# Low parts of sixteen weight tiles by a negated copy and an adding DMA, in a hybrid decoder block on one core

## The chip, the cores and the metric

One core of a Trainium2 chip runs the whole kernel in one launch. The metric is the device time in microseconds (us), the median of several executions. A profiled execution gives the trace; its times count from the start of its span.

The engines by the names used here: TensorE (PE) multiplies, and loads its weights beside that (PEld); VectorE (DVE), ScalarE (ACT) and GpSimd (POOL) work element by element; SyncE (SP) issues most transfers. POOL and ACT issue transfers too, each on a queue of its own.

## The reference, cut to what matters

```python
u = rmsnorm(h, g_mix); z = u @ w_in
...
y_a = o @ w_o_nsa                                # o: attention output
y_b = c @ w_conv_out + b_conv_out                # c: convolution branch
h = h + (ga * y_a + gb * y_b) @ w_out
v = rmsnorm(h, g_ffn) @ w_up
v = causal_dwconv(v, ffn_conv_w, ffn_conv_b)
v_gate, v_val = jnp.split(v, 2, axis=-1)
h = h + (jax.nn.gelu(v_gate) * v_val) @ w_down
gate = jax.nn.sigmoid(rmsnorm(h, g_ple) @ w_ple_gate)
h = h + gate * (p @ w_ple)
return rmsnorm(h, g_final)
```

One sequence of 1024 rows, model width 1024, FFN width 2816, p of width 256, all in float32.

## The kernel before, in words

**Products in two parts.** A float32 product is made of fast products of rounded operands. Each operand is split into a high part, its value rounded to the format that PE takes (`F32R`), and a low part, the value minus the high part. Three matmuls follow for each step: high by high, high by low, low by high (`mm3`, and written out with `mm`, line 169). The low part of a weight is so needed by one matmul in three.

**Weights.** A queue of weight tiles is fixed in advance by `add_w`, in the order of their use: 32 tiles of w_in (z), w_conv_out (co), w_o (o, four tiles), p and w_ple (p and pl), and the 22 chunks of the gate half of w_up (up). The tiles here are 128x1024, 512 KB. `w_fetch` (lines 86 to 93) keeps up to two fetches ahead on SP's queue, into a pool `wp` with two buffers for raw tiles (tag "wr"): a third tile can be fetched only when the first has been read. `w_split` (lines 95 to 108) takes a raw tile and makes the parts: one copy on ACT into the high part (line 102), which rounds, and two subtractions of 512 columns, raw minus high, into the low part (lines 103 to 105). These run on `lo_eng[0]`, VectorE at the start and from the end of the attention on, GpSimd during attention. Names in the rows: wr is a raw tile, wh a high part, wl a low part; the high and low parts of most weights have two buffers each (tags "wh" and "wl").

**Stages around the change.** After the attention come y_b and y_a (w_o, eight column chunks in four tiles). Then the product with w_out, in the seven products of a Strassen-like scheme (`o_steps`), with three of the four pieces of p @ w_ple (`pw_steps`, lines 970 to 989) woven between; a piece stores its result with a transfer issued by POOL (pw_d, line 987). `norm_a` makes the sums of squares and scaled rows of the next norm (lines 182 to 187, f in the rows) and stores h (h_d) by POOL; `norm_b` and `norm_c` transpose them on PE (line 198) and split the sums that the seven FFN products need (T and S in the rows, lines 1178 and 1179, 1195 to 1207). Then the FFN up product, chunk after chunk: `gen` makes the operands, `prod` multiplies. The chunks up 0 to up 3 start early, between the norms, with the fourth piece of p @ w_ple after the first of them (`EARLY`, `NE`); from chunk 4 on there is a regular loop. The x rows that `o_steps` loads are f<-in_x_dram; x in the names of PE's rows is an operand of the w_out product.

**What sets the order.** The program is written as calls woven by hand (`weave`), and a scheduler with a timeline of its own then orders the instructions of every engine (`schedule_with_timeline_sim`). Each engine runs its list in order and waits where an operand or a buffer isn't ready.

Of the kernel before, what the change touches and what calls it, by code (L numbers as in the profile page):

```python
# [11 lines left out]
AF = mybir.ActivationFunctionType  # L12
ALU = mybir.AluOpType
# [21 lines left out]
def tile_hybrid_block(ctx: ExitStack, tc: tile.TileContext, a: dict, out: bass.AP):  # L35
    nc = tc.nc
# [9 lines left out]
    def nm(s):  # L46
        cnt[0] += 1
        return f"{s}{cnt[0]}"
# [37 lines left out]
    lo_eng = [nc.vector]  # L86

    def w_fetch():
        while order and len(raws) < AHEAD:
            key, src, n, pl, th, tl = order.pop(0)  # L90
            raw = wp.tile([128, n], F32, tag="wr", name=nm("wr"))
            nc.sync.dma_start(raw if len(src.shape) == 2 else raw.rearrange("p (c n) -> p c n", c=src.shape[1]), src)
            raws.append((key, raw, n, pl, th, tl))

    def w_split():

        w_fetch()
        if raws and raws[0][3] in pools:
            key, raw, n, pl, th, tl = raws.pop(0)
            hi = pools[pl].tile([128, n], F32R, tag=th, name=nm("wh"))  # L100
            lo = pools[pl].tile([128, n], F32R, tag=tl, name=nm("wl"))
            nc.scalar.activation(hi, raw, AF.Copy)  # L102
            for c0 in range(0, n, 512):
                cs = slice(c0, min(c0 + 512, n))
                lo_eng[0].tensor_tensor(lo[:, cs], raw[:, cs], hi[:, cs], op=ALU.subtract)  # L105
            raw_of[key] = raw
            made.append((key, (hi, lo)))

    def w_get(key):
        while not made:  # L110
            assert order or raws, key
            w_split()
        k, w = made.pop(0)
        assert k == key, (k, key)
        return w
# [24 lines left out]
    EARLY, NE = (3,), 4  # L140
# [135 lines left out]
    def zsteps(z, w, th, nk=8, src=None, split=1):  # L276

        wh, wl = w
        srcs = src or u

        def step(k):
            sl = slice(128 * k, 128 * k + 128)
            movs = []
            for h in th:
                hi, lo = srcs[h][k // 2]
                movs.append((hi[:, k % 2], lo[:, k % 2]))
            mm3([z[h] for h in th], wh[:, sl], wl[:, sl], movs, k == 0, k == nk - 1)
            if k == split:
                w_split()

        return [(lambda k=k: step(k)) for k in range(nk)]
# [254 lines left out]
    for j, nk in enumerate((3, 3, 2)):  # L546
        hi, lo = w_get(("v", j))
# [6 lines left out]
    def v_tile(i):  # L554
        zv = tt_()
        th, t0 = divmod(i, 4)
        for k in range(8):
            uh, ul = u[th][k // 2]
            uh = uh[:, k % 2, 128 * t0:128 * t0 + 128]
            ul = ul[:, k % 2, 128 * t0:128 * t0 + 128]  # L560
            mm(zv[:, 0:280], uh, wv[k][0], k == 0, False)
            mm(zv[:, 0:280], uh, wv[k][1], False, False)
            mm(zv[:, 0:280], ul, wv[k][0], False, k == 7)
        if i == 2:
            w_split()
        for g in range(2):
            vsrc = zv[:, 0:256].rearrange("p (b g d) -> p b g d", b=2, g=2)[:, :, g]
            vd = V[g][i // 4][:, i % 4]
            nc.scalar.activation(vd[:, :, 0:64], vsrc, AF.Copy)
            nc.vector.tensor_sub(vd[:, :, 64:128], vsrc, vd[:, :, 0:64])  # L570
        nc.scalar.activation(gts[:, i], zv[:, 256:280], AF.Tanh, scale=0.5)
# [1120 lines left out]
```

## Time and profile before

| | |
|---|---|
| Median of 3 runs | 1578.37 us (1578.05 to 1578.44) |
| Profiled execution | 1580.51 us |
| Its span | 1578.8 us |
| Mean granted clock of PE | 0.997 |
| DVE, ACT, POOL busy | 77%, 49%, 23% of the span |

The profiled execution stands 2.1 us above the median. The span leaves out 1.7 us at its ends. A busy time adds up the stretches in which an engine worked; an instruction's own time can overlap that of the next on the same engine (a 128x512 matmul takes 0.39 us and the next starts 0.23 us after it). A granted clock of 1.00 is the full 2.4 GHz.

### The profile page before, as it was taken

How to read it: one execution, taken by the hardware profiler on the slowest of the kernel's cores; microseconds unless marked ns; L12 is line 12 of the kernel's file. 1: busy time of each engine (PE TensorE's matmuls, PEld its weight loads, DVE VectorE, ACT ScalarE, POOL GpSimd, SP SyncE). 2: the span in 40 equal slices, each digit the busy share in tenths (PEclk: the TensorE clock that was granted, in tenths of full speed). 3: DMA queues.
4: the chain of work that ended last, by engine and by line, in shares of the span. 5: the costliest groups of instructions: out<-in, count | busy, mean ns of one | idle time of the engine just before them, and what ended most of it. 6: DMA issues, size and time to landing. Idle time of an engine off the chain costs nothing. (4 is left out here: it accounts for less than half of the span.)

```text
span 1578.8 us, 22128 instructions
## 1 busy us (share of the span) xinstructions
PE 1543.1 (98%) x7746; PEld 1305.6 (83%) x7746; DVE 1216.5 (77%) x2342; ACT 780.8 (49%) x1472; POOL 358.0 (23%) x402
## 2 busy tenths in 40 slices
PE   9999999999999999999998999999999989999998
PEld 7888889888988898887876888888888867888886
DVE  4999788577764887779779898898879768778554
ACT  5113324467755776614556454454554456554332
POOL 2000004566663576500120111211111100000000
PEclk9999999999999999999999999999999999999999
DMA  4123233211123431465143232232322499454321
GB/s 165 63 97 124 71 122 142 74 54 55 41 95 122 159 134 68 145 229 187 61 179 134 87 114 87 102 125 81 120 107 87 149 328 311 163 175 133 105 76 54
DMA packets 76048, 194.40 MB, mean 123 GB/s; under 512 B 8481, under 2 KB 8865, under 8 KB 75937
## 3 DMA queue, kind: packets, MB, share of 16 engines
q1 hardware_dynamic: 57184, 146.58, 26.5%
q10 hardware_dynamic: 14400, 31.20, 5.3%
q0 software_dynamic: 4352, 15.21, 2.6%
q8 instruction: 61, 1.00, 0.2%
q14 instruction: 51, 0.41, 0.1%
HBM read 140.26 MB, written 52.69 MB: 122 GB/s over the span
## 5 line engine op out<-in xcount | busy, mean ns | idle before, releaser
L169 PE MATMUL t<-T,S 128*128 128x512 f32 x1320 | 310.4, 390 | 2.2 <-DVE T L1179 1.3
L169 PEld LDWEIGHTS t<-T,S 128*128 128x128 f32 x1320 | 247.5, 188 | 55.4 <-DVE T L1179 2.2
L169 PE MATMUL t<-u,wh 128*128 128x512 f32 x1024 | 288.7, 392 | 0.4 <-DVE u L274 0.3
L169 PEld LDWEIGHTS t<-u,wh 128*128 128x128 f32 x1024 | 189.1, 188 | 36.9 <-DVE ms L252 0.6
L169 PE MATMUL t<-wh,a 128*128 128x512 f32 x616 | 191.8, 392 | 4.2 <-ACT wh L1453 4.2
L169 PE MATMUL t<-u,wl 128*128 128x512 f32 x512 | 167.0, 392 | 0.0
L102 ACT ACTIVATE wh<-wr 128x1024 fp32r<-128x1024 f32 (+1 forms) x72 | 75.5, 1050 | 172.6 <-PE t L169 111.5
L707 POOL TENSOR_TENSOR S<-S,r 128x512 f32<-128x512 f32 (+1 forms) x152 | 140.6, 951 | 60.6 <-DVE r L727 39.0
L336 DVE SCALAR_TENSOR_TENSOR s<-s,cw,s 128x1019 f32<-128x1019 f32 (+16 forms) x120 | 151.6, 1267 | 2.9
L169 PEld LDWEIGHTS t<-wh,a 128*128 128x128 f32 x616 | 116.0, 189 | 29.6 <-ACT wh L1453 5.7
L1337 POOL TENSOR_TENSOR f<-f,f 128x1024 f32<-128x1024 f32 x21 | 57.2, 2726 | 358.2 <-DVE f L1367 227.9
L169 PE MATMUL t<-wl,a 128*128 128x512 f32 x308 | 120.4, 393 | 2.5 <-DVE wl L1454 2.5
L169 PE MATMUL t<-T,wh 128*128 128x512 f32 x352 | 112.8, 393 | 2.3 <-ACT S L1202 1.8
L166 DVE TENSOR_TENSOR P<-t,P 128x512 fp32r<-128x512 f32 (+1 forms) x168 | 97.2, 593 | 22.9 <-ACT P L165 22.0
L165 ACT ACTIVATE P<-t 128x512 fp32r<-128x512 f32 (+1 forms) x168 | 84.2, 524 | 53.8 <-PE t L763 44.1
L169 PEld LDWEIGHTS t<-u,wl 128*128 128x128 f32 x512 | 95.4, 188 | 18.5
L169 PE MATMUL t<-P,v 128*128 128x256 f32 x528 | 102.9, 296 | 0.5 <-ACT P L165 0.2
L722 ACT ACTIVATE S<-S,ngm 128x640 f32<-128x640 f32 (+7 forms) x128 | 93.1, 732 | 13.7 <-DVE ngm L717 13.5
L1297 ACT ACTIVATE S<-s 128x512 fp32r<-128x512 f32 x88 | 54.3, 627 | 76.0 <-PE t L169 47.9
L105 DVE TENSOR_TENSOR wl<-wr,wh 128x512 fp32r<-128x512 f32 x108 | 70.8, 696 | 25.6 <-ACT wh L102 25.3
L169 PE MATMUL t<-v,v 128*128 128x512 f32 (+1 forms) x408 | 89.6, 378 | 0.0
L1458 ACT ACTIVATE a<-r 128x512 fp32r<-128x512 f32 x77 | 48.5, 631 | 82.0 <-PE t L169 59.6
(257 smaller groups left out, 2986.5 us busy)
## 6 DMA issues: line engine op xcount, KB each, us to landing
r<-a_d SPq DMA_DIRECT2D x77, 256.0 KB, 3.5
r<-in_w_dn_dram SPq DMA_DIRECT2D x66, 256.0 KB, 4.1
wr<-in_w_z_dram SPq DMA_DIRECT2D x32, 512.0 KB, 3.6
f<-in_w_up_dram SPq DMA_DIRECT2D x26, 512.0 KB, 3.4
wr<-in_w_up_dram SPq DMA_DIRECT2D x22, 512.0 KB, 3.2
a_d<-f ACTq DMA_DIRECT2D x41, 256.0 KB, 2.1
a_d<-s ACTq DMA_DIRECT2D x30, 256.0 KB, 2.1
s<-in_x_dram SPq DMA_DIRECT2D x8, 512.0 KB, 7.7
```

Source lines behind the costliest of these rows:

```text
L102: nc.scalar.activation(hi, raw, AF.Copy)
L105: lo_eng[0].tensor_tensor(lo[:, cs], raw[:, cs], hi[:, cs], op=ALU.subtract)
L165: nc.scalar.activation(hi, ps, AF.Copy)
L166: nc.vector.tensor_sub(lo, ps, hi)
L169: nc.tensor.matmul(o, l, r, start=s, stop=e, skip_group_check=True)
L336: nc.vector.scalar_tensor_tensor(ac[:, s:], c[:, :T - s], cw2[:, w0 + 30 - s:w0 + 31 - s], ac[:, s:], op0=ALU.mult, op1=ALU.add)
L707: nc.gpsimd.tensor_tensor(d, d, un.r.unsqueeze(2).to_broadcast([128, 2, d.shape[2]]), op=ALU.mult)
L722: nc.scalar.activation(un.S[:, h, 0:nk], un.S[:, h, 0:nk], AF.Exp, bias=un.ngm[:, h:h + 1], accum_out=un.sm[:, h:h + 1])
L1297: nc.scalar.activation(hi, src, AF.Copy)
L1337: (nc.gpsimd if j < NF - 1 else nc.vector).tensor_tensor(o, zg[j], o, op=ALU.mult)
L1458: nc.scalar.activation(hi, x, AF.Copy)
```

## The change

In `w_split`, the tiles of w_o, p and w_ple and the up chunks 0 to 4 get their low part in another way. After the copy into the high part, ACT copies the high part with a scale of -1 into the low part's buffer. POOL then issues a transfer that adds the raw tile, element by element, to what stands in that buffer: raw minus high. The two subtractions are left out. The tiles of z and co and the up chunks from 5 on keep them, now at line 110.

```diff
@@ -100,9 +100,14 @@
             hi = pools[pl].tile([128, n], F32R, tag=th, name=nm("wh"))
             lo = pools[pl].tile([128, n], F32R, tag=tl, name=nm("wl"))
             nc.scalar.activation(hi, raw, AF.Copy)
-            for c0 in range(0, n, 512):
-                cs = slice(c0, min(c0 + 512, n))
-                lo_eng[0].tensor_tensor(lo[:, cs], raw[:, cs], hi[:, cs], op=ALU.subtract)
+            if key[0] in ("o", "p", "pl") or key[0] == "up" and key[1] <= NE:
+
+                nc.scalar.activation(lo, hi, AF.Copy, scale=-1.0)
+                nc.gpsimd.dma_start(lo, raw, accum_op=ALU.add)
+            else:
+                for c0 in range(0, n, 512):
+                    cs = slice(c0, min(c0 + 512, n))
+                    lo_eng[0].tensor_tensor(lo[:, cs], raw[:, cs], hi[:, cs], op=ALU.subtract)
             raw_of[key] = raw
             made.append((key, (hi, lo)))
```

These are sixteen tiles: four of w_o, the first of p, w_ple 0 and 1, the second of p, w_ple 2, up 0, the second of p again, w_ple 3, and up 1 to 4. Lines after 102 move down by five. The change of the costs also moves instructions, as three places show.

PE's list at the first product of p and w_ple (wh_7804 and wl_7805 are the parts of p, wh_7811 and wl_7812 those of w_ple 0; x_7780 to x_7834 and wh_7778, wl_7779 are operands of the w_out product). Before, the four high products stand ahead of sixteen x products, of which five are shown:

```order
L169 MATMUL t_7800<-wl_7779,x_7780 128x512
L169 MATMUL t_7823<-wh_7811,wh_7804 128x512
L169 MATMUL t_7853<-wh_7811,wh_7804 128x512
L169 MATMUL t_7873<-wh_7811,wh_7804 128x512
L169 MATMUL t_7923<-wh_7811,wh_7804 128x512
L169 MATMUL t_7788<-wh_7778,x_7781 128x512
L169 MATMUL t_7788<-wh_7778,x_7833 128x512
L169 MATMUL t_7788<-wl_7779,x_7833 128x512
L169 MATMUL t_7788<-wh_7778,x_7834 128x512
L169 MATMUL t_7792<-wh_7778,x_7781 128x512
```

With the change:

```order
L174 MATMUL t_7800<-wh_7778,x_7833 128x512
L174 MATMUL t_7800<-wl_7779,x_7833 128x512
L174 MATMUL t_7800<-wh_7778,x_7834 128x512
L174 MATMUL t_7823<-wh_7811,wh_7804 128x512
L174 MATMUL t_7853<-wh_7811,wh_7804 128x512
L174 MATMUL t_7873<-wh_7811,wh_7804 128x512
L174 MATMUL t_7923<-wh_7811,wh_7804 128x512
L174 MATMUL t_7823<-wl_7812,wh_7804 128x512
L174 MATMUL t_7823<-wh_7811,wl_7805 128x512
```

The four high products have moved behind the sixteen x products, and stand directly ahead of the first product with wl_7812.

ACT's list around the high copy of w_ple 3 (wr_8772 is its raw tile, wh_8781 its high part; T and S are parts for the FFN products). Before:

```order
L1321 ACTIVATE f_8696<-t_8683 128x512
L182 ACTIVATE f_8857,ss_8858<-f_8163 128x1024
L102 ACTIVATE wh_8781<-wr_8772 128x1024
L1202 ACTIVATE S_8717<-t_8698 128x512
L1178 ACTIVATE T_8673<-S_8711 128x4x128
L1178 ACTIVATE T_8675<-S_8708 128x4x128
L1178 ACTIVATE T_8677<-S_8717 128x4x128
L1178 ACTIVATE T_8675<-S_8752 128x4x128
```

With the change:

```order
L1207 ACTIVATE S_8717<-t_8698 128x512
L187 ACTIVATE f_8857,ss_8858<-f_8163 128x1024
L1183 ACTIVATE T_8673<-S_8711 128x4x128
L102 ACTIVATE wh_8781<-wr_8772 128x1024
L1183 ACTIVATE T_8675<-S_8708 128x4x128
L1183 ACTIVATE T_8675<-S_8752 128x4x128
L1207 ACTIVATE S_8761<-t_8742 128x512
L105 ACTIVATE wl_8782<-wh_8781 128x1024
L1183 ACTIVATE T_8677<-S_8717 128x4x128
```

The high copy stands behind one T copy, and the negation (wl_8782) behind two more T copies and an S copy. Before, the low part wasn't in this list.

SP's fetches from the second tile of p on, with what each waits for (DVE and Activation are the engines' own counters, DMAHW the transfers of SP, DMASW those that POOL issues). Before:

```order
L92 DMA wr_7816<-in_p_t_dram 128x1024 [waits DMAHW6_49,DVE_49,Activation_49]
L92 DMA wr_7961<-in_w_pl_dram 128x1024 [waits DMAHW5_49,DMAHW7_49,DVE_49,Activation_49]
L92 DMA wr_8118<-in_w_up_dram 128x1024 [waits DMAHW0_49,DMAHW6_49,DVE_49,Activation_49]
L92 DMA wr_8125<-in_p_t_dram 128x1024 [waits DMAHW1_49,DMAHW7_49,DVE_49,Activation_49]
L92 DMA wr_8772<-in_w_pl_dram 128x1024 [waits DMAHW0_49,DMAHW2_49,DVE_49,Activation_49]
```

With the change:

```order
L92 DMA wr_7816<-in_p_t_dram 128x1024 [waits DMAHW6_49,DMASW7_49,Activation_49]
L92 DMA wr_7961<-in_w_pl_dram 128x1024 [waits DMAHW5_49,DMAHW7_49,DMASW4_49,Activation_49]
L92 DMA wr_8118<-in_w_up_dram 128x1024 [waits DMAHW0_49,DMAHW6_49,DMASW5_49,Activation_49]
L92 DMA wr_8125<-in_p_t_dram 128x1024 [waits DMAHW1_49,DMAHW7_49,DMASW6_49,Activation_49]
L92 DMA wr_8772<-in_w_pl_dram 128x1024 [waits DMAHW0_49,DMAHW2_49,DMASW7_49,Activation_49]
```

The order is the same; in place of DVE every fetch waits for a transfer of POOL.

## Rows read from the trace of the kernel before

**Rows 1.** Busy time of each engine over the whole span (the page, part 1).

```profile
PE 1543.1 (98%) x7746; PEld 1305.6 (83%) x7746; DVE 1216.5 (77%) x2342; ACT 780.8 (49%) x1472; POOL 358.0 (23%) x402
```

**Rows 2.** Busy time by stretch: length, then each engine (instructions), PEclk, DMA share, GB/s.

```profile
723.80:735.50 11.70, 9.78 (x41) 7.47 (x42) 11.70 (x21) 3.86 (x8) 0.28 (x1) 1.00 0.68 256
735.50:790.00 54.50, 54.50 (x242) 45.16 (x241) 42.22 (x71) 27.56 (x49) 6.86 (x13) 1.00 0.20 78
790.00:815.60 25.60, 25.40 (x129) 21.19 (x128) 18.60 (x30) 13.96 (x24) 4.24 (x8) 1.00 0.47 164
815.60:861.10 45.50, 37.86 (x166) 29.00 (x165) 43.77 (x73) 28.99 (x49) 7.72 (x12) 0.96 0.41 151
861.10:911.00 49.90, 49.65 (x218) 40.76 (x219) 41.78 (x55) 26.66 (x38) 5.10 (x2) 1.00 0.28 100
```

**Rows 3.** The chain of waits, 815 to 862 us: start, length, engine, tile, line.

```profile
818.89 3.67 DVE f L187 x3
...
827.41 1.20 DVE wl L105 x2
...
861.12 0.96 PE t L169 x3
```

**Rows 4.** Line 105: all on DVE (min/median/max ns), then DVE and POOL time in two stretches.

```profile
L105 DVE TENSOR_TENSOR wl<-wr,wh x108: 201/684/2884, 11.8 to 1209.8; 128x512 fp32r<-128x512 f32 x105, 128x328 fp32r<-128x328 f32 x2, 128x48 fp32r<-128x48 f32 x1
...
723.80:735.50 11.70, 2.56 (x4) 0.00 (x0) 1.00 0.68 256
815.60:861.10 45.50, 7.60 (x12) 0.00 (x0) 0.96 0.41 151
```

**Rows 5.** PE's timeline: start, length, line, tiles, count [idle time before <- what ended it].

```profile
730.82 0.50 PE L169 MATMUL t<-wl,wh 128*128 128x512 f32 x1 [1.51 <-DVE wl L105]
...
745.46 1.98 PE L169 MATMUL t<-wh,x 128*128 128x512 f32 x8
...
815.64 0.62 PE L169 MATMUL t<-T,wh 128*128 128x512 f32 x2
...
820.32 1.07 PE L198 MATMUL t<-ident,f 128*128 128x128 f32 x8 [1.80 <-DVE f L187]
...
828.06 0.50 PE L169 MATMUL t<-wl,wh 128*128 128x512 f32 x1 [1.30 <-DVE wl L105]
...
838.52 0.63 PE L169 MATMUL t<-T,wl 128*128 128x512 f32 x1
```

**Rows 6.** ACT's timeline at the first p tile and from p 1 on.

```profile
718.95 1.16 ACT L1079 ACTIVATE x<-m 128x512 fp32r<-128x512 f32 x2 [1.74 <-PE t L169]
...
789.86 1.06 ACT L102 ACTIVATE wh<-wr 128x1024 fp32r<-128x1024 f32 x1 [0.37 <-PE t L169]
...
795.99 1.06 ACT L102 ACTIVATE wh<-wr 128x1024 fp32r<-128x1024 f32 x1 [0.74 <-DMA wr<-in_w_up_dram]
...
806.79 0.60 ACT L986 ACTIVATE s<-t 128x512 f32<-128x512 f32 x1 [4.57 <-DMA pw_d<-s]
```

**Rows 7.** DMA issues: destination <- source, queue, count, KB each, median us to landing.

```profile
wr<-in_w_up_dram SPq DMA_DIRECT2D x22, 512.0 KB, 3.2
...
f<-in_x_dram SPq DMA_DIRECT2D x8, 512.0 KB, 7.4
pw_d<-s POOLq DMA_DIRECT2D x16, 256.0 KB, 2.5
h_d<-f POOLq DMA_DIRECT2D x8, 512.0 KB, 4.0
...
o<-o_d POOLq DMA_DIRECT2D x4, 512.0 KB, 7.5
```

**Rows 8.** POOL's timeline, two stores issued one after the other.

```profile
832.23 1.13 POOL L987 DMA_DIRECT2D pw_d<-s  x2 [7.93 <-ACT s L986]
```

**Rows 9.** Busy time by stretches of 10 us, columns as in rows 2.

```profile
830.00:840.00 10.00, 7.36 (x31) 5.28 (x30) 10.00 (x18) 8.45 (x15) 2.21 (x4) 0.92 0.33 130
840.00:850.00 10.00, 10.00 (x42) 8.18 (x41) 10.00 (x18) 5.01 (x8) 0.00 (x0) 0.91 0.37 127
```

## The prediction

> **What bounds the kernel now.** I read the busy shares first, then busy time by stage, then the chain that ended last, then the timelines of the stretches where TensorE (PE) is not full. PE is busy for 98% of the span [rows 1], so a change elsewhere can only win where PE waits, and can lose anywhere. The stages that hold the 16 touched tiles show where it waits: nearly full from 735.5 to 815.6 and after 861.1, but busy for 37.86 us of the 45.50 between 815.6 and 861.1, where VectorE (DVE) is busy for 43.77, and for 9.78 of the 11.70 between 723.8 and 735.5, where DVE is busy throughout [rows 2]. The chain agrees: from 818.89 to 861.12 it runs mostly over DVE, subtractions of line 105 among it [rows 3]. So the kernel is PE's, with two holes dug by DVE. What can be won is 7.64 + 1.92 us of idle PE, and 1.8 us for the granted clock of 0.96 in the longer stretch: 11.4 us.
>
> **The change: what goes.** 16 tiles lose two 128x512 subtractions each. Four of the 32 (w_o 0 and 1) run on POOL during attention, 28 on DVE at 0.68 [rows 4]. Twelve line-105 instructions with 7.60 us lie in the long hole [rows 4]; two belong to up chunk 5 and stay, so 6.3 us of DVE work leave it.
>
> **What comes.** Sixteen 128x1024 negations on ScalarE (ACT). Of that shape a high-part copy takes 1.06 us [rows 6], some 0.95 of it until the next one starts. ACT is busy for 28.99 of the 45.50 us of the long hole [rows 2]: there is room, but each negation stands in line with other copies. Then sixteen transfers of POOL. To issue one costs POOL about 0.55 us (two in 1.13) [rows 8]; POOL is nearly idle there, which hides it. The landing is the price: no row shows an adding transfer. From below it is 3.2 us, what SP's plain 512 KB loads take; from above 7.5, the worst plain 512 KB of POOL's queue, plus 1.4 for the old low part, which must be read too: 8.9 [rows 7]. (1.4 us: 256 KB take 2.5 us on POOL's queue and 512 KB 3.2 on SP's, so 0.7 for 256 KB more.) I take **5.4**: 4.0 of h_d<-f, the nearest row (same queue, same size, from SBUF), plus 1.4.
>
> The Trainium skill's page "DMA: Bandwidth & Descriptors", section "Anatomy of one DMA — SWDGE (gpsimd) path", puts a transfer of this path at 2.0 us plus its bytes at 436 GB/s. An estimate from it: 3.2 us for 512 KB, 4.4 when both operands are read. The rows are above it, since a plain 512 KB takes 4.0 on this queue. By 4.4 the sum below, at the 4.3 us per us given there, would be 9.5 instead of 13.8, and the time 1587.9.
>
> A low part so comes 1.0 + 5.4 = 6.4 us after its high copy where two subtractions gave it after 1.2 to 1.3. PE runs its list in order, so this costs wherever no other PE work stands between. Place by place, in the times of the profiled run:
>
> *w_o, from 598 to 716.* PE has high-part products and other chunks ahead; I found several us between landing and use for all four. Cost 0, hidden by the products of the previous w_o tile; without that cover each would cost up to 5.
>
> *First p and w_ple (the short hole).* From 718.95 on [rows 6] the new ACT list has three copies of m, the p copy, three more copies, the negation of p, the w_ple copy and its negation: six of 0.55 and four of 0.95, that is until about 726.3. Plus 5.4 is 731.7. But the eight loads of x are under way, which take 7.4 us where an undisturbed 512 KB load takes 3.2 [rows 7]; I add 1.8 and get 733.5. PE arrives at 729.3 in the old run and waits 1.51 us for line 105 [rows 5]; with the four high products moved behind the sixteen x products it arrives at 729.5. It goes on at 733.5 instead of 730.82: **+2.7**.
>
> The Trainium skill's same page, section "Issuing engines are not separate DMA queues", says that transfers of SP, ACT and POOL run on the same 16 engines and interleave; that speaks against the change at this place. The 7.4 us agree with it.
>
> *p 1, w_ple 2, up 0, second p (790 to 815).* Only two raw tiles exist, and a fetch now waits for the adding transfer that reads the tile before last, no more for DVE. The p copy of 789.86 [rows 6] leads to a negation until 792.5, a landing at 798.0, and only then the fetch of up 0 (3.2 us [rows 7], 0.4 for the steps between): it arrives at 801.6, where it came for 795.99 [rows 6]. The next pair (negation until 795.7, POOL's pow, landing at 801.6) puts the second p at 805.2, its copy and negation until 807.2. Behind them in ACT's list stand the pw copies of the second product; the last of these needs a free tile, that is a pw_d store of 2.5 us [rows 7], until about 811, where its counterpart ran at 806.79 [rows 6]. The squares and eight T copies follow, some 8 us, so up 0 starts on PE near 819.2 instead of 815.64 [rows 5]. The transposes that then stand in up 0 find their rows ready, which saves the 1.8 us in which PE waited there in the old run. At the end of up 0 I get 826.7 against 825.0: 1.7 us behind.
>
> *w_ple 3.* Its high copy needs the tile of up 0, so 828.2; ACT then does two T copies and an S copy and the negation, until 830.9; landing 836.4. PE has three high products and the 16 transposes until 829.8, then waits 6.6 us. Old: 828.06 [rows 5]. Behind: 8.3, less one product (0.23 us, eight in 1.98 [rows 5]) done early, 8.1.
>
> *up 1.* The high copies of up 1 and up 2 wait for the end of that product, 841.2; two copies, two T copies and the negation end at 845.4, the landing is 850.8. PE has eight high products and eight transposes as cover, until about 844, and waits 6 to 7 us. Old: 838.52 [rows 5]. Behind: 12.3 less four products, 11.4.
>
> *up 2 to up 4.* Covered: up 2 lands while up 1 runs, up 3 has 25 products ahead, up 4 is due in the main loop. Here DVE's 6.3 us pay back: the old run lost 1.9 us in waits from 856 to 861 and about 1.7 at a low clock (0.92 and 0.91 in the two slices of 10 us from 830 on [rows 9]), which no longer come on top. Behind: 11.4 - 3.6 = **+7.9** with rounding. From 861.1 on PE is busy for 49.65 of 49.90 us, so nothing is made up later.
>
> *Clock.* The granted clock fell between its two levels (2.4 and 1.2 GHz) right after the gaps of PE from 834 to 838, at a price of about 1.7 us [rows 9]. The two new gaps of over 6 us should each bring such a fall: **+3.2**.
>
> **Sum:** 2.7 + 7.9 + 3.2 = 13.8 us. The profiled execution took 1580.5 (span 1578.8), 2.1 over the median of 1578.37; against the median, **1592.2 us**, 0.9% slower. Three landings follow one another on this path (the second w_ple 2's, then w_ple 3's and up 1's), and the first place adds one more: a landing longer or shorter by 1 us is worth about 4.3 us. At 3.2 us, walking the same list, the late part comes to +2, the first place to -1.2, without falls of the clock: +1. At 8.9 it is 10.6 + 15 + 5 = +31.
>
> **Rivals.** (a) *DVE's relief wins: faster.* For it: DVE is full in both holes and the chain runs over it [rows 2, 3]; 6.3 us of its work and 2.6 in the short hole go. Against it: the same low parts stay due, later. It decides when the landing is under about 2.9 us; half of the 11.4 us that can be won is then the likely gain: 1572.7. (b) *Latency eats relief: no change.* Landing at 3.2 to 3.4 us, as plain loads: 1578 to 1581. (c) *The transfer is far slower than a copy*, by reading and adding in POOL's queue one after another: 7.5 to 8.9, 1602 to 1609. For it: POOL's own 512 KB loads at 7.5 [rows 7]; against it: h_d at 4.0. (d) That the change doesn't do what it says can be left out: the built program holds the 16 transfers, and PE's list waits for them.
>
> **How the numbers follow.** Forecast with landings from 3.5 to 7.4 us: 0.58, by itself 1581 to 1601. Rival (c): 0.15. Rival (b): 0.12. Rival (a): 0.15. A measurement of this kernel tells 0.2%, 3.2 us, from no change. Faster 0.15, same 0.12, slower 0.73. The range of 8 in 10 takes part of (a) and nearly all of (c): 1573 to 1607.
>
> **What would show it.** The wait list of PE should have DMA wl in place of DVE wl, in three long gaps: 2 to 6 us near 730, and 5 to 8 us each before the low products of w_ple 3 and up 1; between issue and landing of wl<-wr some 5.4 us. DVE should drop to about 36 us of the stretch that corresponds to the long hole, and PE's busy share there fall. Wrong would be: landings of 3 us or less, no wait of PE for wl, or long waits at w_o, which I hold covered.

## The result, and the profile after

The changed kernel takes 1599.7 us in the median (1597.37 to 1600.01, 4 runs), the kernel before 1578.4 (1578.05 to 1579.16). The ratio is 1.0128, with a 95% interval from 1.0116 to 1.0140: slower by 20.2 us, where 13.8 were forecast. (The two medians stand 21.3 us apart; the text goes by the ratio on record.) The profiled execution took 1599.87 us, its span 1598.1, which is 19.3 more than before. Here "+x us" is always against the kernel before: the ratio, by its runs, for a whole kernel, and the profiled execution for a place.

The engines over the whole span, after (the page, part 1; before: [rows 1]):

```profile
PE 1549.9 (97%) x7746; PEld 1311.8 (82%) x7746; DVE 1199.2 (75%) x2314; ACT 796.1 (50%) x1488; POOL 370.2 (23%) x414
```

DVE lost 17.3 us and ACT gained 15.3, as the change says. PE has the same 7746 matmuls and is busy for 6.8 us longer, at a lower clock: the busy time of each slice of 4 us, multiplied by the share that is missing of the full clock, adds up to 2.8 us before and 10.8 after. The idle time of PE, its span less its busy time, rose from 35.7 to 48.2 us.

The places show in busy time by stretch. The cuts are the same points of PE's list in both traces: the end of the w_o products, of the first p and w_ple product, of the w_out product, and of w_ple 3 (columns as in rows 2). Before:

```profile
671.00:720.00 49.00, 49.00 (x225) 40.82 (x224) 37.57 (x63) 8.93 (x17) 2.56 (x3) 1.00 0.58 213
720.00:735.50 15.50, 13.46 (x58) 10.18 (x57) 15.50 (x27) 7.57 (x14) 0.28 (x1) 1.00 0.75 283
735.50:815.60 80.10, 79.90 (x369) 66.35 (x368) 60.82 (x100) 41.52 (x72) 11.10 (x20) 1.00 0.29 105
815.60:833.90 18.30, 14.80 (x74) 11.39 (x74) 16.57 (x27) 11.74 (x22) 6.82 (x11) 1.00 0.49 186
833.90:913.90 80.00, 75.52 (x323) 60.34 (x322) 71.88 (x104) 44.21 (x66) 6.32 (x5) 0.98 0.29 106
913.90:1578.80 664.90, 650.61 (x2908) 537.51 (x2906) 505.31 (x707) 319.46 (x512) 65.37 (x42) 1.00 0.39 137
```

After:

```profile
671.40:724.30 52.90, 51.05 (x226) 42.06 (x225) 33.77 (x57) 11.70 (x19) 3.51 (x5) 0.97 0.68 227
724.30:745.40 21.10, 14.74 (x56) 11.09 (x56) 17.87 (x30) 10.64 (x17) 2.91 (x5) 0.92 0.85 275
745.40:822.90 77.50, 77.50 (x349) 64.24 (x348) 47.23 (x75) 41.38 (x67) 14.66 (x23) 1.00 0.38 111
822.90:854.60 31.70, 21.16 (x94) 16.78 (x93) 28.50 (x47) 20.23 (x38) 7.74 (x12) 0.78 0.55 198
854.60:934.60 80.00, 74.59 (x319) 60.41 (x318) 58.90 (x81) 44.61 (x64) 9.37 (x8) 0.96 0.44 130
934.60:1598.10 663.50, 649.67 (x2912) 537.00 (x2910) 503.93 (x708) 319.12 (x512) 69.42 (x42) 1.00 0.39 137
```

The w_o stretch grew from 49.0 to 52.9 us, the short hole from 15.5 to 21.1, the next two together from 98.4 to 109.2 (some twenty matmuls, mostly transposes, have moved across the cut between them, so they are read as one). The two rows of 80 us behind w_ple 3 are of one length by choice, so a loss shows there as less work: PE is busy for 74.59 us against 75.52, 0.9 less, although DVE is busy for 58.90 there instead of 71.88. What follows is 1.4 shorter. With 0.4 us that were lost ahead of 671.4, 3.9 + 5.6 + 10.8 + 0 - 1.4 make the 19.3. Not all of this is the change's: the clock fell at 605 us only after, behind a gap of PE of 1.97 us that both traces have, and at 1289 us only before, and these falls cost 1.6 and 1.4 us.

The transfers themselves: DMA issues after, and the smallest, median and largest landing of line 106:

```profile
wl<-wr POOLq DMA_DIRECT2D x16, 512.0 KB, 5.4
```

```profile
DMA to landing us min/median/max: 4.4/5.4/10.6
```

PE's timeline after, the five long waits of these stretches:

```profile
700.64 0.73 PE L174 MATMUL t<-o,wl 128*128 128x512 f32 x2 [1.85 <-DMA wl<-wr]
...
739.41 0.79 PE L174 MATMUL t<-wl,wh 128*128 128x512 f32 x1 [4.38 <-DMA wl<-wr]
...
829.95 0.80 PE L174 MATMUL t<-T,wh 128*128 128x512 f32 x1 [3.38 <-ACT T L1183]
...
848.00 0.79 PE L174 MATMUL t<-wl,wh 128*128 128x512 f32 x1 [5.22 <-DMA wl<-wr]
...
863.26 0.79 PE L174 MATMUL t<-T,wl 128*128 128x512 f32 x1 [4.06 <-DMA wl<-wr]
```

POOL's timeline after, the issues that four of them waited for (w_o 2, w_ple 0, w_ple 3, up 1):

```profile
689.95 0.88 POOL L106 DMA_DIRECT2D wl<-wr  x1 [8.69 <-ACT wl L105]
...
732.87 0.86 POOL L106 DMA_DIRECT2D wl<-wr  x1 [1.19 <-DMA f<-in_x_dram]
...
843.48 0.91 POOL L106 DMA_DIRECT2D wl<-wr  x1 [3.19 <-ACT wl L105]
...
858.75 0.88 POOL L106 DMA_DIRECT2D wl<-wr  x1 [3.96 <-ACT wl L105]
```

From issue to PE's next matmul it is 10.7 us at w_o 2, 6.5 at w_ple 0, and 4.5 each at w_ple 3 and up 1. The fifth wait, at up 0, is told by the chain of waits after, in order of time:

```profile
802.56 4.39 DMA wl<-wr
...
807.01 4.77 DMA wr<-in_w_up_dram
...
816.82 0.51 POOL wl L106
...
817.36 5.31 DMA pw_d<-s
...
825.93 1.46 ACT T L1183 x3
...
828.43 1.47 ACT T L1183 x3
...
829.95 0.80 PE t L174
```

The landing of the second p's transfer frees a raw tile, and only then SP fetches up 0. ACT's high copy of it starts at 811.81, before at 795.99 [rows 6]; less the 9.9 us that PE is behind by then, that is 5.9 us later. Behind it in ACT's list come its negation, and the copy and the negation of the second p, which is fetched again; POOL issues its transfer, and then the pw_d store that ACT needs before it can copy the next product. That store takes long in both kernels, 5.31 us here; before, one was issued at 801.54 and ACT waited for it until 806.79 [rows 6]. The squares and T copies follow, and PE starts up 0 at 829.95.

Behind each wait stands a stretch at a lower clock (slices of 4 us after; PEclk is the third number from the right):

```profile
700.00:704.00 4.00, 3.36 (x9) 2.71 (x10) 0.00 (x0) 0.00 (x0) 0.00 (x0) 0.66 1.05 289
...
740.00:744.00 4.00, 4.00 (x14) 3.21 (x13) 2.17 (x4) 1.20 (x2) 0.58 (x1) 0.72 0.44 137
828.00:832.00 4.00, 2.05 (x8) 1.88 (x9) 4.00 (x8) 2.38 (x6) 1.31 (x2) 0.50 1.01 394
848.00:852.00 4.00, 4.00 (x10) 3.19 (x11) 4.00 (x8) 1.63 (x4) 0.56 (x1) 0.57 0.40 131
864.00:868.00 4.00, 4.00 (x11) 3.13 (x10) 0.80 (x2) 1.64 (x4) 0.00 (x0) 0.50 1.04 273
```

1.00 is 2.4 GHz and 0.50 is 1.2 GHz; a matmul of 0.39 us took 0.63 there. Before, only one such fall lies in these stretches [rows 9], behind this wait:

```profile
837.90 0.82 PE L169 MATMUL t<-T,wh 128*128 128x512 f32 x2 [1.84 <-ACT S L1202]
```

### The profile page after: what moved, and what is told of

It is laid out like the page before. It is cut to its first block, busy times and chain, and to the rows that moved or that the text cites. A ratio compares the mean times of both kernels' runs of the same rounds, so it can differ in the third digit from the quotient of the medians.

```text
span 1598.1 us, 22140 instructions
## 1 busy us (share of the span) xinstructions
PE 1549.9 (97%) x7746; PEld 1311.8 (82%) x7746; DVE 1199.2 (75%) x2314; ACT 796.1 (50%) x1488; POOL 370.2 (23%) x414
## 4 chain that ended last, share of the span: by engine, by line
PE 85%; DMA 5%; DVE 4%; issue 3%; ACT 2%; POOL 0%; SPq 0%; POOLq 0%; ACTq 0%; DVEq 0%
PE t L174 81%; PE t L768 3%; DMA wl<-wr 2%; DMA f<-h_d 1%; PE t L203 1%; DMA s<-in_x_dram 1%; DMA r<-in_w_dn_dram 1%; DVE S L699 0%; DMA f<-in_gains_dram 0%; DVE f L1370 0%; DMA pw_d<-s 0%; DVE f L1372 0%; DVE S L1303 0%; DMA wr<-in_w_up_dram 0%; ACT f L1369 0%
## 5 line engine op out<-in xcount | busy, mean ns | idle before, releaser
L1342 POOL TENSOR_TENSOR f<-f,f 128x1024 f32<-128x1024 f32 x21 | 60.9, 2901 | 340.1 <-DVE f L1372 199.0
L1369 ACT ACTIVATE f<-f,cv 128x1024 f32<-128x1024 f32 x44 | 54.6, 1241 | 66.4 <-DVE f L1328 48.7
```

The lines of the kernel that those rows point to most:

```text
L1342: (nc.gpsimd if j < NF - 1 else nc.vector).tensor_tensor(o, zg[j], o, op=ALU.mult)
L1369: nc.scalar.activation(o, z, AF.Identity, bias=cv[:, C_FB + c:C_FB + c + 1], scale=cv[:, wc + 2:wc + 3])
```

## The theories

**A, the landing.** PE reaches a low part before its adding transfer has landed, and the low clock behind each wait comes on top. **B, the bulk.** The sixteen extra ACT instructions, and the order that the scheduler gives the program with them, cost wherever they stand. **C, the raw tile.** It is held until the landing, and the next fetch is what comes late. **D.** The effects of the tile groups just add up. A got a rider after the first four runs: a delay ahead of the long hole is given back there, since DVE catches up while PE waits, so what the hole costs can be saved once only.

## The experiments

All are edits of the changed kernel.

**w_o alone.**

```diff
-            if key[0] in ("o", "p", "pl") or key[0] == "up" and key[1] <= NE:
+            if key[0] == "o":
```

> Theory A (the time goes where PE reaches a low part before its adding transfer has landed, and in the low clock after each such wait): at w_o one wait of 1.85 us was seen and 1.3 to 2 us of low clock behind it, so about +4 us over the kernel before, with a landing near 10 us for the third w_o tile, beside the eight loads of w_ot. Theory B (the two extra instructions per tile and the moved order cost, wherever they stand): a quarter of the tiles, a quarter of the 21 us, some +5 us, without a wait of PE for wl. Theory C (the raw tile is held longer, and the next fetch is what comes late): +4 us too, but with PE waiting for a high part behind a late fetch.

Ratio 1.0025 (1.0015 to 1.0034), +3.9 us. PE waits for wl, for less than with all sixteen tiles; the landings ran from 6.0 to 9.7 us. PE's timeline:

```profile
701.03 0.73 PE L174 MATMUL t<-o,wl 128*128 128x512 f32 x2 [0.89 <-DMA wl<-wr]
...
725.92 0.50 PE L174 MATMUL t<-wh,x 128*128 128x512 f32 x1 [1.01 <-ACT x L1084]
...
729.38 1.19 PE L174 MATMUL t<-wh,wh 128*128 128x512 f32 x4 [1.35 <-ACT wh L102]
```

The size is that of A and of C, the places are mostly others. The wait for wl is 0.89 us, and no fall of the clock follows it. More is lost at the first p and w_ple product, to copies of ACT, whose list has moved. A high part is late there, as C has it, but not through its fetch: the raw tile had landed at 710.8, and ACT took it up at 728.3. This is B's kind of cost. Where the rest of the 3.9 us lies wasn't followed up.

**p and w_ple alone.**

```diff
-            if key[0] in ("o", "p", "pl") or key[0] == "up" and key[1] <= NE:
+            if key[0] in ("p", "pl"):
```

> Theory A: waits for wl at the first p and w_ple product and at w_ple 3 (4.4 and 5.2 us with all sixteen tiles), 1.5 to 2 us of low clock behind each, so +9 to +13 us. Theory B: seven of sixteen tiles, about +9 us, spread. Theory C: the fetch of up 0 still comes late behind the second p tile's transfer, and up 0 starts late by about 5 us, although up 0 itself is subtracted: of the +9 to +13 us at least 4 lie between the end of the w_out product and the end of up 0.

1.0072 (1.0055 to 1.0089), +11.4 us. PE's timeline, at w_ple 0 and w_ple 3:

```profile
736.94 0.80 PE L174 MATMUL t<-wl,wh 128*128 128x512 f32 x1 [6.08 <-DMA wl<-wr]
...
844.93 0.80 PE L174 MATMUL t<-wl,wh 128*128 128x512 f32 x1 [4.90 <-DMA wl<-wr]
```

The end of w_ple 3 comes 17.4 us late, counted from the same matmul at 604 us, and 6 to 7 of these are given back behind it. This is where the rider comes from.

**The up chunks alone.**

```diff
-            if key[0] in ("o", "p", "pl") or key[0] == "up" and key[1] <= NE:
+            if key[0] == "up" and key[1] <= NE:
```

> Theory A: one wait of 4 us for wl at up 1 and up to 2 us of low clock, less the waits on DVE that the kernel before has from 835 to 861 us (4.4 us) and its low clock there (1.7 us): 0 to +3 us. Theory B: five of sixteen tiles, +6 to +7 us. Theory C: +4 or more, since the fetches of w_ple 3 and of up 1 to 3 wait for transfers.

0.9970 (0.9960 to 0.9981), 4.7 us *faster* than before, outside what any theory gave. No wait for a transferred wl is left in PE's list; at up 1 it waits for an S copy of ACT that stands in line behind two negations:

```profile
841.59 2.74 PE L174 MATMUL t<-T,wh 128*128 128x512 f32 x6 [3.73 <-ACT S L1207]
```

**ACT's part without the transfer.**

```diff
-                nc.gpsimd.dma_start(lo, raw, accum_op=ALU.add)
+                for c0 in range(0, n, 512):
+                    cs = slice(c0, min(c0 + 512, n))
+                    lo_eng[0].tensor_tensor(lo[:, cs], raw[:, cs], lo[:, cs], op=ALU.add)
```

> The negated copies on ACT stay, all sixteen, but VectorE (GpSimd for the first two) adds the raw tile in two halves instead of the transfer. Theory A: the low part comes 1 to 2 us later than in the kernel before and no landing is waited for: +1 to +5 us, no wait over 3 us for wl. Theory B (ACT's copies and the moved order are the price): most of the +21 us stays, +12 or more. Theory C: as A, since the raw tile is freed by DVE again.

0.9971 (0.9959 to 0.9983), 4.6 us faster than before. PE's two largest groups of waits over the whole span (total, times, longest):

```profile
PE t L176 <- DVE wl L108: 4.7, 2, 2.4
PE t L176 <- ACT S L1209: 3.7, 1, 3.7
```

B falls as the main cause: with all sixteen negations in ACT's list and a new order, nothing of the 20 us is there. It is the transfer that costs. The gain wasn't foreseen, and it lies outside A's +1 to +5 too; it comes back below.

**All but the up chunks.**

```diff
-            if key[0] in ("o", "p", "pl") or key[0] == "up" and key[1] <= NE:
+            if key[0] in ("o", "p", "pl"):
```

> w_o, p and w_ple by transfer, the up chunks subtracted. Measured alone, w_o costs 3.9 us over the kernel before, p and w_ple 11.3 (1591.57 less 1579.52 is 12.1, by the ratio 11.4), up gains 4.7; all together 20.2. Theory A with one rider (the time that VectorE's full stretch costs behind w_ple 3 is lost once: either PE's lateness lets VectorE catch up there, or the transfers take its work away, and then up 1's own landing is left as a cost): +14 to +16 us, so that the up chunks, which gain 4.7 alone, cost about 5 us here. Theory D (all effects add up, and the rest of the 20 us is another place): +20 or more, since the up chunks only gain.

1.0056 (1.0039 to 1.0072), +8.8 us, less than even the rider gave, and far from D's 20. The 80 us behind w_ple 3:

```profile
854.60:934.60 80.00, 79.72 (x354) 65.26 (x353) 70.40 (x99) 44.59 (x66) 10.54 (x5) 1.00 0.30 108
```

PE is busy for 79.72 of 80 us, where the kernel before has 75.52 and the change 74.59. PE comes 20 us late to this stretch, DVE has caught up, and the hole is gone. The same up chunks that gain 4.7 us alone so cost 11 here.

**All but up 1.**

```diff
-            if key[0] in ("o", "p", "pl") or key[0] == "up" and key[1] <= NE:
+            if key[0] in ("o", "p", "pl") or key[0] == "up" and key[1] <= NE and key[1] != 1:
```

> All of the change but for up chunk 1, which is subtracted. Theory A with the rider: the wait of 4.1 us at up 1 and the 2.6 us of low clock behind it go, +13 to +16 us. Theory D: as with all sixteen tiles, +19 to +21.

1.0084 (1.0069 to 1.0099), +13.3 us: A with the rider. The same 80 us:

```profile
853.90:933.90 80.00, 77.00 (x340) 62.54 (x339) 65.15 (x89) 45.05 (x67) 12.55 (x8) 1.00 0.40 124
```

77.00 us busy, at full clock: up 1 is worth 2.4 us of busy time there, and its clock.

**From HBM.**

```diff
-                nc.gpsimd.dma_start(lo, raw, accum_op=ALU.add)
+                nc.gpsimd.dma_start(lo if len(src.shape) == 2 else lo.rearrange("p (c n) -> p c n", c=src.shape[1]), src,
+                                    accum_op=ALU.add)
```

(`w_fetch` and `w_split` hand `src` on with the raw tile.)

> The transfer adds the weight out of HBM in place of the raw tile in SBUF, so a raw tile is free again after the high copy, and the next fetch needn't wait for a landing. The landing itself stays about as long (4.5 to 6 us). Theory A (what costs is the low part's own lateness, four times): the fetches come 5 us sooner, but three of the four waits stay; up 0 starts some 4 us sooner: +13 to +18 us. Theory C (the late fetches are most of it): +8 or less.

1.0199 (1.0182 to 1.0216), +31.4 us. The premise failed. Landings of line 106:

```profile
DMA to landing us min/median/max: 5.1/8.1/11.6
```

The median rose from 5.4 to 8.1. So C isn't tried cleanly, but it is weak: no fetch waits for a landing any more, and the kernel is slower by 11.2 us. At up 0, where the late fetch stands in the chain, PE's wait fell only from 3.38 to 2.15 us. The 11.2 us give no price per us of landing, since the median is over tiles most of which PE doesn't wait for. Where it does, at w_o 2, w_ple 0, w_ple 3 and up 1, the landings went from 10.6, 6.5, 4.5 and 4.5 us to 10.5, 8.7, 5.4 and 5.1, and at up 3 a new wait of 3.83 us came, with a fall of the clock.

**In halves.**

```diff
-                nc.gpsimd.dma_start(lo, raw, accum_op=ALU.add)
+                for c0 in range(0, n, 512):
+                    nc.gpsimd.dma_start(lo[:, c0:c0 + 512], raw[:, c0:c0 + 512], accum_op=ALU.add)
```

> Each transfer is split into two of 512 columns, 256 KB each. Theory A: if a half lands a microsecond or more sooner than the whole (a plain store of 256 KB lands after 2.5 us where 512 KB took 4.0 to 5.4), PE goes on sooner at all four places, +12 to +17 us; if the second half lands when the whole did, nothing changes, +19 to +23. Theory C: as A, the raw tile is freed by the second half.

1.0120 (1.0105 to 1.0135), +19.0 us, the same as whole. Landings of the halves:

```profile
DMA to landing us min/median/max: 3.2/4.6/10.4
```

A half lands 0.8 us sooner in the median, and the end of w_ple 3 came 3.6 us sooner than with whole transfers, which is A's size. But 5.0 were lost again behind it: 1.6 in further idle time and 3.0 at a low clock from 930 us on. Where those came from wasn't followed up.

**The up chunks, added by VectorE.** Only the up chunks, with the addition of the fourth experiment.

```diff
-            if key[0] in ("o", "p", "pl") or key[0] == "up" and key[1] <= NE:
+            if key[0] == "up" and key[1] <= NE:
...
-                nc.gpsimd.dma_start(lo, raw, accum_op=ALU.add)
+                for c0 in range(0, n, 512):
+                    cs = slice(c0, min(c0 + 512, n))
+                    lo_eng[0].tensor_tensor(lo[:, cs], raw[:, cs], lo[:, cs], op=ALU.add)
```

> Only the up chunks 0 to 4 are changed, and VectorE adds the raw tile to the negated copy instead of a transfer, so VectorE has as much to do as in the kernel before. Rival R (the 4.6 us that the up chunks gain by transfer are VectorE's relief): within 1 us of the kernel before, or slower. Rival O (they come from the order that the scheduler gives once ACT holds the negations, above all PE's early products of up 2 and the first steps of the down product): 3 to 5 us faster, as with the transfers.

0.9996 (0.9987 to 1.0006), -0.6 us, as rival R said; but R's reason doesn't hold. Busy time behind w_ple 3, and at the start of the down product. The up chunks added by VectorE:

```profile
834.70:914.70 80.00, 75.58 (x323) 61.38 (x321) 72.12 (x104) 47.99 (x70) 6.89 (x5) 0.96 0.29 107
1270.00:1340.00 70.00, 64.64 (x271) 51.37 (x270) 56.40 (x88) 44.23 (x76) 3.27 (x6) 0.98 0.93 336
```

The up chunks by transfer:

```profile
835.60:915.60 80.00, 75.71 (x329) 61.68 (x328) 70.40 (x100) 49.56 (x72) 12.47 (x9) 0.98 0.45 133
1270.00:1340.00 70.00, 66.97 (x289) 53.21 (x288) 61.60 (x96) 44.96 (x77) 3.30 (x6) 1.00 0.95 345
```

Behind w_ple 3 PE is busy alike, 75.58 and 75.71 us, and as in the kernel before. DVE is busy for 1.7 us less there with the transfers, and PE's busy time shows nothing of it; that PE gets 329 matmuls into the 80 us instead of 323 fits its clock, 0.98 against 0.96. Both kernels have the same wait of 3.73 us for an S copy of ACT at up 1, with VectorE relieved and without, so it goes with the negations. The difference in time lies 430 us later, 64.64 against 66.97. There the kernel before, and the fourth experiment:

```profile
1270.00:1340.00 70.00, 63.35 (x264) 49.80 (x263) 56.15 (x87) 44.07 (x74) 3.27 (x6) 0.98 0.95 332
```

```profile
1270.00:1340.00 70.00, 67.05 (x288) 53.18 (x287) 60.81 (x95) 44.74 (x77) 3.27 (x6) 1.00 0.95 343
```

The two kernels that gain have 3.6 us more of PE there. The order of the instructions differs there too. In the traces of the two kernels that gain, SP's first loads of the down product (and ACT's copies of them, and a few rows of PE's) stand in another order, SP's the same in both; in the traces of all other kernels here this part of SP's list stands as in the kernel before. So most of the 4.6 us goes with an order of loads that the scheduler chose, and neither with relief nor with cover at the up chunks. Which of those rows matters wasn't tried. Rival O had the right place, but this kernel doesn't get that order.

**Mixed.** The transfer for the up chunks, VectorE's addition for the rest.

```diff
-                nc.gpsimd.dma_start(lo, raw, accum_op=ALU.add)
+                if key[0] == "up":
+                    nc.gpsimd.dma_start(lo, raw, accum_op=ALU.add)
+                else:
+                    for c0 in range(0, n, 512):
+                        cs = slice(c0, min(c0 + 512, n))
+                        lo_eng[0].tensor_tensor(lo[:, cs], raw[:, cs], lo[:, cs], op=ALU.add)
```

> All sixteen tiles with the negated copy; the five up chunks by transfer, the others added by VectorE (GpSimd for the first two). Theory A: no transfer stands where PE waits for it, and nothing of the 20 us is left; 3 to 7 us faster than the kernel before, faster than either part alone only if relief and order are two things. If transfers of the up chunks cost by themselves wherever ACT holds other negations (Theory B): slower than the 4.6 us gain by 3 or more.

1.0005 (0.9996 to 1.0014), +0.8 us. Nothing of the 20 us is left, as A has it, but neither is the gain, so A's 3 to 7 us faster are missed; SP's loads of the down product are in the old order again:

```profile
1270.00:1340.00 70.00, 64.42 (x270) 50.40 (x269) 54.12 (x85) 45.60 (x76) 3.30 (x6) 0.98 0.94 332
```

**The first p and w_ple alone.**

```diff
-            if key[0] in ("o", "p", "pl") or key[0] == "up" and key[1] <= NE:
+            if key in (("p", 0), ("pl", 0)):
```

> Only the first p tile and w_ple 0 by transfer. Theory A: PE waits 4 to 6 us for wl at their first low product, near 735 us, with 1 to 1.5 us of low clock behind it; it has over 70 us of full PE work behind it before VectorE's full stretch, and keeps the delay until there: +3 to +7 us in all. Theory B (a share per tile): +2.5 us and no long wait.

1.0056 (1.0041 to 1.0071), +8.8 us, more than A's range. PE's timeline and the two landings:

```profile
737.93 0.80 PE L174 MATMUL t<-wl,wh 128*128 128x512 f32 x1 [6.27 <-DMA wl<-wr]
```

```profile
DMA to landing us min/median/max: 8.4/8.9/9.3
```

Issued at 726.1 and 728.6, while the x loads run, both took twice the 4.5 us of an undisturbed one. The place sets the price and not the number of tiles: two tiles cost as much as B's share for seven. The run also limits the rider: of the 10.3 us that PE is late at the end of w_ple 3, counted as above, 9.2 are left at the end of the kernel. What is lost there, so far ahead of the long hole, is hardly given back.

**w_ple 3 alone.**

```diff
-            if key[0] in ("o", "p", "pl") or key[0] == "up" and key[1] <= NE:
+            if key == ("pl", 3):
```

> Only w_ple 3 by transfer. Theory A with the rider: PE waits 4 to 6 us for wl at w_ple 3, 1 to 2 us of low clock follow, and VectorE catches up meanwhile, so that most is given back in the stretch behind it: the end of w_ple 3 comes 5 to 7 us later, the end of the kernel 0 to 3 us. Without the rider (delays add up): +5 to +7 at the end too. Theory B: +1.3 us.

0.9993 (0.9984 to 1.0002), -1.1 us. The end of w_ple 3 came 6.1 us late, and the kernel no later than before. But the delay is hardly the landing's: 1.2 us of it lie ahead of the hole, and in place of the 4 to 6 us for wl PE waited 3.0 us for an S copy, ahead of a high product, and 0.8 for wl; a fall of the clock followed. The 80 us behind it:

```profile
839.70:919.70 80.00, 78.60 (x348) 64.03 (x346) 71.51 (x101) 43.43 (x65) 10.52 (x5) 1.00 0.31 107
```

78.60 us busy at full clock, 3.1 more than before: the delay is given back, as the rider has it, on a single tile and whatever made it.

## Why the prediction was right, and where its size was off

**Direction and mechanism: right.** Three long waits for wl were named, 2 to 6 us near 730 and 5 to 8 each at w_ple 3 and up 1; the first two are 4.38 and 5.22, and the third, with 4.06, is a little short. The late fetch of up 0 was named too: its tile was put at 801.6, where ACT had taken it up at 795.99, 5.6 us later, and it came 5.9 later. The change costs because PE reaches low parts before their transfers have landed: the kernel with all sixteen negations and no transfer has nothing of the 20 us.

**The landing: 5.4 forecast, 5.4 in the median, which is luck.** The median mixes undisturbed landings, 4.4 to 4.6 us, with those beside other transfers, up to 10.6. Where PE waits it is 6.5 at w_ple 0, with 7.2 forecast, and 4.5 each at w_ple 3 and up 1, with 5.4 forecast. The Trainium skill's page "DMA: Bandwidth & Descriptors", section "Anatomy of one DMA — SWDGE (gpsimd) path", puts a transfer at 2.0 us plus its bytes at 436 GB/s, from which the prediction worked out an estimate of 4.4 us with both operands read; the landings at w_ple 3 and up 1 agree with it. The same page of the Trainium skill, section "Issuing engines are not separate DMA queues", says that transfers of all engines run on the same 16 DMA engines and interleave; the 10.6 us at w_o 2 agree with it. No run shows the 4.3 us per us of landing. The issue of a transfer was put at 0.55 us and takes POOL 0.88.

**Waits: 12.2 us forecast, 12.5 measured.** The terms without the clock are 2.7 at the first place and 11.4 at up 1, less the old waits of 1.9; PE's idle time rose by 12.5. That the sum is met so well is luck too, since the places aren't: 1.9 at w_o for 0, 4.3 for 2.7 at the first p and w_ple, 6.8 for 8.1 at up 0 and w_ple 3, 0.9 for 1.4 behind, and 1.5 less in the rest.

**Clock: 3.2 forecast for two falls, 9.2 measured in five.** This is the term that was most off. The five cost 1.5, 1.2, 2.3, 1.7 and 2.5 us. Falls were counted only for the two gaps of over 6 us, at w_ple 3 and up 1. The trace of before already had one behind a gap of 1.84, and after, the gaps of 1.85, 4.38 and 3.38 us had one each, which the sum put at nothing. The fall that the kernel before had at 838 is gone, as forecast, so that over the whole span the clock costs 8.0 us more, where 3.2 less 1.7 were forecast.

**"Cost 0" at w_o: wrong, +3.9 in this stretch.** The wait is 1.85 us, and the clock behind it costs 1.5. The third tile's transfer was issued amid eight loads of w_ot and took 10.6 us. The cover of other w_o products was there, and it was too short. The prediction knew that x loads stretch a transfer at the next place and didn't ask the same here. The run with w_o alone costs 3.9 us too, but with a wait of 0.89 and mostly at other places.

**First p and w_ple: +2.7 forecast, +5.6 measured.** The wait for wl is 4.38 in place of 1.51, so 2.9 more, as forecast. The rest is two waits of PE for x, of 1.01 us on ACT and 0.96 on DVE, where the kernel before has one of 0.37, and 1.2 us of low clock; neither was in the sum.

**Up 0 and w_ple 3: 8.1 behind forecast, 10.8 measured.** The waits stand where they were put, up 0 for ACT's T copies (3.38) and w_ple 3 for the landing. PE's idle time grew by 6.8 us there, less than forecast; the clock, 0.78 in the mean over 31.7 us, makes up for more than that.

**"DVE's 6.3 us pay back" 3.6: the old losses are gone, but not through the relief.** The 1.9 us of waits from 856 to 861 and the fall at 838 don't come on top, as forecast. But without any up transfer, where DVE keeps the up chunks' subtractions, they are gone too (79.72 us busy of 80): PE's lateness is enough. Up 1's own landing stands in their place (without it 77.00). And when the up chunks are changed alone, and PE is hardly late, it waits 3.73 us for an S copy of ACT, whether a transfer or VectorE does the adding. So the step "what DVE no longer does, PE gets" isn't borne out: work went from the engine that was full to the one that was next.

By stretch the forecast was 0, 2.7, 8.1 and -0.2, and 3.2 for the clock: 13.8. Measured: 3.9, 5.6, 10.8, 0 (with 0.9 us of PE's work less) and -1.4 behind, and 0.4 ahead: 19.3, with the clock in them.

Rival (a), relief wins, falls with the kernel of the up chunks alone, whose relief doesn't show in PE's busy time behind w_ple 3. That kernel beats both, at 1574.92 us, and so does the one without any transfer, at 1574.33; but most of what they win lies at the start of the down product, 430 us away. Rival (b), a landing of 3.2 to 3.4 us, falls with the shortest of 4.4.

## What to carry to other kernels

An operation that moves from a busy engine to a transfer takes its place in time with it: ask of each result how long after its inputs it is used, and what other transfers run in that time, before counting the engine's relief. Delays and reliefs right ahead of a stretch that another engine fills don't add up: try the parts alone and together, and read the stretch behind them. When a part alone costs what it costs in the whole, look whether it costs it at the same place. Where a scheduler orders the program, a gain of a few us may sit hundreds of us away from the edit; look there before crediting the edit.

## What the runs showed of the hardware

An adding transfer of 512 KB from SBUF to SBUF landed after 4.4 us at best and 10.6 at worst, and after 8.1 in the median (5.1 to 11.6) when one operand came out of HBM. To issue one kept POOL for 0.88 us, against 0.53 to 0.59 for a plain store of 256 or 512 KB in the kernel before. Split into two halves it gained the kernel nothing. At each of five idle gaps of PE of 1.85 to 5.22 us the granted clock fell to its lower level, 1.2 GHz (0.50 to 0.72 in the mean of a slice of 4 us), at a price of 1.2 to 2.5 us each. A gap alone doesn't decide it: behind the same gap of 1.97 us at 604.6 us the clock fell in the trace after and not in the one before. The rise of 8.0 us in all is two fifths of what this change costs.
